# Two paddings that shift the activation tiles x and t by 192 and 384 bytes in SBUF

## The chip, the cores and the metric

The kernel runs on one core of one Trainium2 chip. The metric is the device time of one execution in microseconds (us), lower is better. The time before is the median of three runs, 1311.45 us (1309.43 to 1313.15).

## The reference, cut to what matters

The program is a stack of two blocks on 256 tokens (272 with 16 meta tokens in the first block) of 1,024 features, in float32. The first block is two hybrid layers, the second a feed-forward network, a mixer with a state-space branch, a cross attention and a second feed-forward network. Nearly all of the arithmetic lies in products of an activation with a weight matrix:

```
proj = jnp.einsum('btd,de->bte', h, w_in)            # each of the two hybrid layers
gate, up = jnp.split(u @ w_gate_up, 2, axis=-1)      # each of the two feed-forward networks
return (jax.nn.silu(gate) * up) @ w_down
```

## The kernel before

**Products in three parts.** An activation lies with features on the partitions and tokens along the free axis, in tiles of four blocks `[128, 4, n]`, where n is 272 tokens in the two layers and 256 after them. To keep float32 accuracy with the faster float32r matmul, a weight and an activation are each split into two float32r parts that add up to them: `wh` and `wl`, and a high and a low tile of the activation. One block of 128 rows and 128 columns of a weight matrix then takes three matmuls (`mm3`, lines 217 to 219): `wh` times high, `wh` times low, `wl` times high. `product` runs K such blocks into one PSUM region. In each of them the weight part is the stationary operand (128 columns of 4 bytes, 512 bytes per partition) and the activation the moving one (n columns of 4 bytes, so 1,024 or 1,088 bytes per partition). Each matmul has its own weight load, which stands in the profile under PEld.

**Weights.** `load_w` (L179) brings 1 MB of weights on SyncE's queue into one of three buffers `w`. `split_w` makes the parts of half a buffer: ScalarE copies it into `wh` (L195), VectorE subtracts into `wl` (L197). Five halves of parts are held, so ScalarE and VectorE work ahead of TensorE.

**Who is moving.** The normalized input of the layers, of the two gate-and-up products (44 weight tiles), of the first products of the mixer and of the query product is in tiles named x, from pool `xp`. Everything else that is multiplied by weights is in tiles named t, from pools `tp1` and `tp2`. In the value product of the cross attention (L1053 to L1055) the roles are exchanged: two neighbouring blocks of `wh` or `wl` are moving, 1,024 bytes, and a part of t is stationary. L1021 multiplies a t tile by a t tile.

**Where the tiles lie.** Pools are laid out in SBUF in the order in which they are opened, each partition alike: `cp` (constants), `wp` (3 x 8,192 bytes of `w`, 5 x 4,096 of `wh`, 5 x 4,096 of `wl`), `xp` (4 x 4,352), `sp`, `sm`, and then `tp1` with `lp` (first block) or `tp2` with `mp` (second block). In the built program the first `wh` starts at byte 60,256, the first `wl` at 80,736, the first x at 101,216 and the first t at 138,656. Modulo 256 that is 96 for all weight parts and all x, and 160 for all t: x lies 0 bytes and t 64 bytes from the weight parts, modulo 256. A block of a weight part is 512 bytes and a block of a tile of 256 tokens is 1,024, so in the second block of the program every matmul of `mm3` has the same distance, 0 with x and 64 with t. A block of 272 tokens is 1,088 bytes, which is 64 modulo 256: in the two layers the four blocks of a tile run through the four distances 0, 64, 128, 192 in turn. At L1053 to L1055 the moving operand lies at 96 and the stationary at 160, a distance of 192.

**Order.** The program's order is fixed by the order of the code; side work (attention, the state-space chunks, norms) is written as generators, and `product` takes a step of it at its end.

Of the kernel before, what the change touches and what calls it, by code (L numbers as in the profile page):

```python
# [10 lines left out]
F32 = mybir.dt.float32  # L11
# [7 lines left out]
P = 128  # L19
# [5 lines left out]
EPS = 1e-6  # L25
# [30 lines left out]
def plan():  # L56
    """The weight tiles in the order of their use: name, index, blocks of 128 rows and columns."""
    out = []
    for l in range(2):
        out += [(f"in{l}", i, 16) for i in range(19)]  # L60
        out += [(f"yab{l}", i, 16) for i in range(4)]
        out += [(f"out{l}", i, 16) for i in range(4)]
    out += [("gu1", i, 16) for i in range(NFF)]
    out += [("dn1", i, 11) for i in range(16)]
    out += [("in2", i, 16) for i in range(8)] + [("dt", 0, 8)] + [("in2", i, 16) for i in range(8, 40)]
    out += [("oa", i, 16) for i in range(4)]
    out += [("os", i, 16) for i in range(8)]
    out += [("mx", i, 16) for i in range(4)]
    out += [("kv", i, 16) for i in range(4)]
    out += [("wq", i, 16) for i in range(4)]  # L70
    out += [("kv", i, 16) for i in range(4, 8)]
    out += [("wo", i, 16) for i in range(4)]
    out += [("gu2", i, 16) for i in range(NFF)]
    out += [("dn2", i, 11) for i in range(16)]
    return out
# [3 lines left out]
def tile_hybrid_stack(ctx: ExitStack, tc: tile.TileContext, a: dict, out: bass.AP):  # L79
# [3 lines left out]
    cp = ctx.enter_context(tc.tile_pool(name="cp", bufs=1))  # L83
    wp = ctx.enter_context(tc.tile_pool(name="wp", bufs=2))
    xp = ctx.enter_context(tc.tile_pool(name="xp", bufs=4))
    sp = ctx.enter_context(tc.tile_pool(name="sp", bufs=4))
    sm = ctx.enter_context(tc.tile_pool(name="sm", bufs=4))
# [50 lines left out]
    def load_first():  # L138
        """The inputs and the first weights in the order in which they are needed."""
        w = wp.tile([P, 16, P], F32, tag="w", name=nm("w"), bufs=AHEAD)  # L140
        src = a["in0"][0].rearrange("p (b c) -> p b c", c=P)
        nc.sync.dma_start(vec, a["vec"])
        for i in range(4):
            nc.sync.dma_start(hT[:, 2 * i:2 * i + 2], a["xT"][:, 2 * i:2 * i + 2])
            nc.sync.dma_start(w[:, 4 * i:4 * i + 4], src[:, 4 * i:4 * i + 4])
        return w

# [1 line left out]
    side = []  # L149
# [14 lines left out]

# [1 line left out]
    tiles = plan()  # L166
# [34 lines left out]
    def block(name):  # L201
        """The next block of weights."""
        h = st["half"]
        if h < 0 or st["blk"] == halves[h][2] - halves[h][1]:
            st["half"], st["blk"] = h + 1, 0
            parts.pop(h, None)
            h += 1
            while st["split"] < min(h + PARTS, len(halves)):
                split_w()
        assert tiles[halves[h][0]][0] == name, (tiles[halves[h][0]], name)  # L210
        st["blk"] += 1
        return [x[:, st["blk"] - 1] for x in parts[h]]
# [8 lines left out]
    def wide(ws, part):  # L221
        """Two neighbouring blocks as one operand."""
        x, _ = ws[0][part], ws[1][part]
        return bass.AP(tensor=x.tensor, offset=x.offset, ap=[list(x.ap[0]), [1, 2 * P]])

    def product(o, name, x, K):
        """o = the sum of K blocks of the weights, each times a part of x."""
        for k in range(K):
            mm3(o, name, x(k), k == 0, k == K - 1)
        pump(rate[0])  # L230

    def quads(hi, lo, n=None, t0=0):
        """The parts of block k in tiles of four blocks."""
        return lambda k: (hi[k // 4][:, k % 4, t0:n], lo[k // 4][:, k % 4, t0:n])

    def split_x(hi, lo, src, scale=None):
        """hi + lo == src (times a per-partition scale)."""
        if scale is None:
            A.activation(hi, src, AF.Copy)  # L239
            V.tensor_sub(lo, src, hi.bitcast(F32))  # L240
        else:
            A.activation(hi, src, AF.Copy, scale=scale)
            V.scalar_tensor_tensor(lo, src, scale, hi.bitcast(F32), op0=OP.mult, op1=OP.subtract)  # L243

    def rsqrt(src, n, scale):
        """(src * scale + EPS) ** -0.5 for a few columns."""
        x, t, y = small(n), small(n, I32), small(n, I32)
        V.tensor_scalar(x, src, scale, EPS, op0=OP.mult, op1=OP.add)
        V.tensor_scalar(t, x.bitcast(I32), 1, None, op0=OP.logical_shift_right)
        V.tensor_scalar(y, t, -1.0, MAGIC, op0=OP.mult, op1=OP.add)  # L250
        y = y.bitcast(F32)
        for _ in range(3):
            s, r, z = small(n), small(n), small(n)
            V.tensor_mul(s, y, y)
            V.scalar_tensor_tensor(r, s, -0.5, x, op0=OP.mult, op1=OP.mult)
            V.scalar_tensor_tensor(z, r, 1.5, y, op0=OP.add, op1=OP.mult)
            y = z
        return y

    # token tiles: column, first token of the statistics' rows, first token, tokens  # L260
    TILES1 = [(1, META, META, P), (2, META + P, META + P, P), (0, 0, 0, META)]
    TILES2 = [(0, 0, 0, P), (1, P, P, P)]

    def spread(o, r, tiles):
        """Columns over tokens to rows that all partitions hold."""
        for col, _, s, m in tiles:
            PE.matmul(o[:, s:s + m], r[:m, col:col + 1].to_broadcast([m, P]), ident[:m, :m], start=True, stop=True)  # L267

    class Norm:
        """RMS norm over features of an activation [P, 8, n]: the parts of the activation times  # L270
        the gain, and the reciprocal root of the mean square of each token."""

# [40 lines left out]

# [1 line left out]
    ident_b = cp.tile([P, P], BF16, name="ident_b")  # L315

    def layer(l, nrm, nxt):
# [9 lines left out]

        # keys (index and attention), values and index weights
        ps = project(0)
# [38 lines left out]

        # index queries
        def rope(dst, raw):  # L370
            """Two blocks of two heads, turned."""
            ps = pair()
# [28 lines left out]

        # the choice of keys by the index scores
        mb = {}
# [41 lines left out]

        # queries
        q = t4()
# [10 lines left out]
        def finish_q():  # L458
            """The queries' own norm, of each token and head."""
            c0 = 1 if t0 else 0  # L460
            n = 3 - c0
# [15 lines left out]

        # gates: twice the silu
        def gate():
# [9 lines left out]

        # attention over the chosen keys  # L490
        at_h, at_l = t4(dt=F32R), t4(dt=F32R)
# [75 lines left out]

        # pooling over trailing windows of 2, 4, 8, 16 tokens
        u = t4()
# [41 lines left out]

        # merge gates: twice the sigmoid less one
        tm = [t4() for _ in range(4)]
# [49 lines left out]

# [1 line left out]
    phase["tp"] = ctx.enter_context(tc.tile_pool(name="tp2", bufs=20))  # L665
# [30 lines left out]

# [1 line left out]

# [6 lines left out]

    # the normalized activation, for all but the first products
    def normalize():
# [22 lines left out]
    def conv4(c0):  # L730
        """Four blocks of the convolved channels from c0: twice their silu."""
        y, r = t4(S), t4(S)
# [20 lines left out]

    # steps: softplus(raw + bias), on tokens x heads
    dp_ = bank()
# [33 lines left out]
    V.tensor_scalar(dts, dt, 0.125, None, op0=OP.mult)  # L789
    # sums of la up to each token of its chunk  # L790
    acs_d = dp.tile([2, 32, P], F32, name="acs_d")
# [28 lines left out]
    def ssd(g):  # L820
# [11 lines left out]
        for c in range(2):  # L832
# [9 lines left out]
            yield  # L842
        # the first chunk's state, and the second chunk's view of it
        A.activation(ab, ab, AF.Exp)
# [79 lines left out]

    # short convolution branch
    sh, sl = two(S), two(S)
# [43 lines left out]

    # the memory, for the cross attention
    mem = two(S, F32)
# [22 lines left out]

# [1 line left out]
    drain()  # L997
# [20 lines left out]
    def three(o, w, x, start, stop):  # L1018
        """o = the product of two operands in parts."""
        for i, (a_, b_) in enumerate(((0, 0), (0, 1), (1, 0))):  # L1020
# [70 lines left out]

# [1 line left out]
def _pack(w, blocks, m):  # L1093
    """[K, N] -> [tiles, P, m * K/P * P]: tiles of m blocks of columns, P rows of K on partitions."""
    k = w.shape[0] // P
# [5 lines left out]
def _fp(x):  # L1101
    """[n * P] -> [P, n]"""
    return x.reshape(-1, P).T
# [117 lines left out]
```

## Time and profile before

| what | value |
|---|---|
| median of three runs | 1311.45 us |
| runs | 1309.43, 1313.15, 1311.45 us |
| span of the profiled execution, first to last instruction | 1305.1 us |
| TensorE matmul (PE), weight load (PEld) busy | 97%, 93% of the span |
| VectorE (DVE), ScalarE (ACT), GpSimd (POOL) busy | 71%, 50%, 16% |
| mean granted TensorE clock, share of full | 0.990 |
| HBM read, mean rate over the span | 209.47 MB, 161 GB/s |

The page gives the profiled execution's own time as its span; what a run has beyond it, 6.35 us at the median, lies around the program. Matmuls overlap in the pipeline, so the duration shown for one (near 280 ns) is not what it costs. What it costs is the step from its start to the start of the next, and that is read from start times or from the count of matmuls in a stretch without a gap.

### The profile page before, as it was taken

Reading aid. Unit: us, or ns where it says so; the run is one execution under the profiler, and the core shown is the slowest. Engines: PE = TensorE matmul, PEld = TensorE weight load, DVE = VectorE, ACT = ScalarE, POOL = GpSimd, SP = SyncE. Lnnn points to the kernel's source line nnn. Section 1 sums busy time; section 2 is a strip of 40 time slices with the busy share of each in tenths; the row PEclk is TensorE's granted clock in tenths of the full one; section 3 lists DMA queues with packets and bytes.
Section 4 is the critical chain, followed back from the end, with each engine's and each line's share of the span. In section 5 each row is a group of like instructions: output and inputs, shape, how many; then the busy total and the mean of one; then the engine's idle time right before and its main releaser. Section 6 shows DMA issues by size and latency. Waiting matters only on the chain.

```text
span 1305.1 us, 24570 instructions
## 1 busy us (share of the span) xinstructions
PE 1265.1 (97%) x10202; PEld 1211.9 (93%) x10202; DVE 928.6 (71%) x1526; ACT 654.4 (50%) x973; POOL 209.2 (16%) x165
## 2 busy tenths in 40 slices
PE   7999999999999999999999999999999999999996
PEld 6988689998679899999999999899999999999996
DVE  6698467769647676766678798777778677777653
ACT  5344554444554544445566644455456455444452
POOL 3141022224103100000002333330003001000011
PEclk9999999999899999999999999999999999999998
DMA  7433235443215545545654565454555544555451
GB/s 271 150 130 130 97 105 168 156 162 130 97 65 184 171 162 194 176 142 182 230 180 144 196 224 181 154 184 162 193 195 194 166 157 139 185 175 181 144 189 55
DMA packets 32975, 212.13 MB, mean 163 GB/s; under 512 B 3664, under 2 KB 3792, under 8 KB 11232
## 3 DMA queue, kind: packets, MB, share of 16 engines
q1 hardware_dynamic: 31104, 204.77, 45.7%
q0 software_dynamic: 1184, 4.23, 0.9%
q8 instruction: 80, 1.31, 0.4%
q10 hardware_dynamic: 576, 1.57, 0.4%
q14 instruction: 31, 0.25, 0.1%
HBM read 209.47 MB, written 1.08 MB: 161 GB/s over the span
## 4 chain that ended last, share of the span: by engine, by line
PE 79%; DVE 12%; ACT 3%; issue 3%; POOL 2%; DMA 1%; DVEq 0%; SPq 0%; ACTq 0%; POOLq 0%
PE bank L217 19%; PE bank L218 18%; PE bank L219 18%; PE pair L217 5%; PE pair L218 5%; PE pair L219 5%; DVE wl L197 4%; ACT wh L195 2%; PE aux L519 2%; PE aux L500 1%; DVE acc L418 1%; DVE acc L425 1%; PE aux L516 1%; DVE sm L424 1%; PE aux L267 1%
## 5 line engine op out<-in xcount | busy, mean ns | idle before, releaser
L197 DVE TENSOR_TENSOR wl<-w,wh 128x1024 fp32r<-128x1024 f32 (+3 forms) x406 | 494.4, 1220 | 206.6 <-ACT wh L195 203.9
L195 ACT ACTIVATE wh<-w 128x1024 fp32r<-128x1024 f32 (+3 forms) x406 | 410.7, 1015 | 454.0 <-PE bank L218 303.1
L217 PE MATMUL bank<-t,wh 128*128 128x256 f32 x1320 | 372.0, 282 | 0.4 <-ACT t L239 0.4
L219 PE MATMUL bank<-t,wl 128*128 128x256 f32 x1320 | 367.9, 279 | 0.0
L218 PE MATMUL bank<-t,wh 128*128 128x256 f32 x1320 | 367.8, 279 | 0.0
L217 PEld LDWEIGHTS bank<-t,wh 128*128 128x128 f32 x1320 | 248.0, 188 | 1.8 <-issue 0.8
L218 PEld LDWEIGHTS bank<-t,wh 128*128 128x128 f32 x1320 | 247.4, 187 | 0.7 <-issue 0.7
L219 PEld LDWEIGHTS bank<-t,wl 128*128 128x128 f32 x1320 | 247.7, 188 | 0.0
L217 PE MATMUL bank<-x,wh 128*128 128x256 f32 x832 | 235.8, 284 | 1.2 <-DVE hT L644 1.2
L218 PE MATMUL bank<-x,wh 128*128 128x256 f32 x832 | 235.7, 283 | 0.0
L219 PE MATMUL bank<-x,wl 128*128 128x256 f32 x832 | 235.4, 283 | 0.0
L217 PE MATMUL pair<-x,wh 128*128 128x272 f32 (+1 forms) x608 | 183.6, 302 | 9.4 <-ACT wh L195 7.8
L219 PE MATMUL pair<-x,wl 128*128 128x272 f32 (+1 forms) x608 | 178.6, 294 | 0.9 <-DVE wl L197 0.9
L218 PE MATMUL pair<-x,wh 128*128 128x272 f32 (+1 forms) x608 | 178.5, 294 | 0.0
L217 PEld LDWEIGHTS bank<-x,wh 128*128 128x128 f32 x832 | 159.6, 192 | 1.2 <-ACT wh L195 1.2
L218 PEld LDWEIGHTS bank<-x,wh 128*128 128x128 f32 x832 | 159.7, 192 | 0.1
L219 PEld LDWEIGHTS bank<-x,wl 128*128 128x128 f32 x832 | 159.7, 192 | 0.0
L298 POOL TENSOR_TENSOR ss<-ss,s 128x256 f32<-128x256 f32 (+1 forms) x48 | 45.9, 960 | 604.4 <-ACT s L296 604.1
L217 PEld LDWEIGHTS pair<-x,wh 128*128 128x128 f32 x608 | 118.2, 195 | 13.5 <-ACT wh L195 8.0
L219 PEld LDWEIGHTS pair<-x,wl 128*128 128x128 f32 x608 | 118.2, 194 | 1.6 <-DVE wl L197 1.4
L218 PEld LDWEIGHTS pair<-x,wh 128*128 128x128 f32 x608 | 118.1, 194 | 0.8 <-DVE x L243 0.2
L217 PE MATMUL pair<-t,wh 128*128 128x272 f32 (+1 forms) x256 | 73.4, 288 | 3.5 <-DVE hT L644 2.4
(259 smaller groups left out, 1617.9 us busy)
## 6 DMA issues: line engine op xcount, KB each, us to landing
w<-in_in SPq DMA_DIRECT2D x77, 1024.0 KB, 4.9
w<-in_gu SPq DMA_DIRECT2D x44, 1024.0 KB, 4.9
w<-in_dn SPq DMA_DIRECT2D x32, 704.0 KB, 4.1
w<-in_yab SPq DMA_DIRECT2D x8, 1024.0 KB, 4.9
w<-in_out SPq DMA_DIRECT2D x8, 1024.0 KB, 5.0
w<-in_os SPq DMA_DIRECT2D x8, 1024.0 KB, 4.9
w<-in_kv SPq DMA_DIRECT2D x8, 1024.0 KB, 4.9
t<-acs_d POOLq DMA_DIRECT2D x8, 512.0 KB, 5.4
```

The source lines that it names most:

```text
L195: A.activation(hi[:, b:b + step], w[:, b:b + step], AF.Copy)
L197: (G if slow else V).tensor_sub(lo[:, b:b + step], w[:, b:b + step], hi[:, b:b + step].bitcast(F32))
L217: PE.matmul(o, wh, xh, start=start, stop=False)
L218: PE.matmul(o, wh, xl, start=False, stop=False)
L219: PE.matmul(o, wl, xh, start=False, stop=stop)
L267: PE.matmul(o[:, s:s + m], r[:m, col:col + 1].to_broadcast([m, P]), ident[:m, :m], start=True, stop=True)
L298: G.tensor_add(self.sum, self.sum, self.last)
L418: V.scalar_tensor_tensor(acc[:, :nk], x[:, :nk], wcol, acc[:, :nk], op0=OP.mult, op1=OP.add)
L424: V.max(out=m8, in_=acc[:, :nk])
L425: V.match_replace(out=acc[:, :nk], in_to_replace=m8, in_values=acc[:, :nk], imm_value=MARK)
L500: PE.matmul(lg[:, :nk], q[64 * e:64 * e + 64, i, s0:s0 + P], kk[64 * e:64 * e + 64, 1, :nk], start=True, stop=False)
L519: PE.matmul(po[64 * e:64 * e + 64], vt[:m, c, :HD], ptt[:m], start=c == 0, stop=c == qt)
```

## The change

Two pools of one tile of 48 float32 (192 bytes per partition) are opened, one ahead of `xp` and one behind it. Nothing reads or writes the two tiles. All that lies behind moves up: x by 192 bytes, and `sp`, `sm`, t, `lp` and `mp` by 384 bytes. In the built program of the change x starts at 101,408 and t at 139,040, both 32 modulo 256, while `wh` and `wl` stay at 96. The distance of x and of t from the weight parts is then 192 modulo 256 (at L1053 to L1055 it becomes 64, since there the roles are exchanged). Two t tiles keep their distance from each other, and so do t and the tiles of `lp` (such as `kk`). Every engine's instructions and their order stay as they are. The rest of the diff takes out comments and docstrings.

```diff
     cp = ctx.enter_context(tc.tile_pool(name="cp", bufs=1))
     wp = ctx.enter_context(tc.tile_pool(name="wp", bufs=2))
+    before_x = ctx.enter_context(tc.tile_pool(name="before_x", bufs=1))
+    before_x.tile([P, 48], F32, name="pad_x")
     xp = ctx.enter_context(tc.tile_pool(name="xp", bufs=4))
+    after_x = ctx.enter_context(tc.tile_pool(name="after_x", bufs=1))
+    after_x.tile([P, 48], F32, name="pad_s")
     sp = ctx.enter_context(tc.tile_pool(name="sp", bufs=4))
     sm = ctx.enter_context(tc.tile_pool(name="sm", bufs=4))
```

## Rows read from the trace of the kernel before

**Rows 1.** The page: busy share, and the chain that ended last, by engine.

```profile
PE 1265.1 (97%) x10202; PEld 1211.9 (93%) x10202; DVE 928.6 (71%) x1526; ACT 654.4 (50%) x973; POOL 209.2 (16%) x165
...
PE 79%; DVE 12%; ACT 3%; issue 3%; POOL 2%; DMA 1%; DVEq 0%; SPq 0%; ACTq 0%; POOLq 0%
```

**Rows 2.** TensorE by line and form: count, busy us, mean ns, idle before.

```profile
L217 PE MATMUL bank<-t,wh 128*128 128x256 f32 x1320 | 372.0, 282 | 0.4 <-ACT t L239 0.4
L217 PE MATMUL bank<-x,wh 128*128 128x256 f32 x832 | 235.8, 284 | 1.2 <-DVE hT L644 1.2
...
L217 PE MATMUL pair<-x,wh 128*128 128x272 f32 x352 | 107.5, 305 | 9.4 <-ACT wh L195 7.8 <-DVE mp L538 1.0 <-DVE r L377 0.6
...
L217 PE MATMUL pair<-x,wh 128*128 128x256 f32 x256 | 76.2, 298 | 0.0
...
L1053 PE MATMUL bank<-wh,t 128*128 128x256 f32 x64 | 18.2, 284 | 0.0
```

**Rows 3.** Stretches: length, busy us and count by engine, clock, DMA share, GB/s.

```profile
464.00:575.00 111.00, 111.00 (x928) 111.00 (x927) 79.09 (x90) 49.88 (x59) 0.00 (x0) 1.00 0.49 169
576.00:638.00 62.00, 62.00 (x528) 62.00 (x528) 40.39 (x50) 32.35 (x49) 4.78 (x6) 1.00 0.61 202
835.30:848.40 13.10, 13.10 (x118) 13.10 (x118) 13.10 (x28) 6.32 (x9) 3.28 (x1) 1.00 0.43 136
1119.00:1230.00 111.00, 111.00 (x928) 111.00 (x927) 78.63 (x90) 49.78 (x58) 0.00 (x0) 1.00 0.50 169
```

**Rows 4.** Stretches with products of t, TensorE alone: length, busy us, count.

```profile
744.30:758.00 13.70, 13.70 (x123) 1.00 0.80 295
781.50:792.50 11.00, 11.00 (x99) 1.00 0.52 177
826.30:831.00 4.70, 4.70 (x44) 1.00 0.56 193
832.10:834.40 2.30, 2.30 (x23) 1.00 0.83 223
835.30:848.40 13.10, 13.10 (x118) 1.00 0.43 136
861.60:872.00 10.40, 10.40 (x94) 1.00 0.50 159
1079.80:1101.30 21.50, 21.50 (x192) 1.00 0.44 147
```

**Rows 5.** Timeline of the value product, its first stretch: start us, duration.

```profile
1042.61 0.28 PE L1053 MATMUL bank<-wh,t 128*128 128x256 f32 x1
...
1044.73 0.88 PE L1021 MATMUL aux<-t,t 128*128 128x256 f32 x6
```

**Rows 6.** Timeline of the value product, a later stretch.

```profile
1045.80 0.28 PE L1053 MATMUL bank<-wh,t 128*128 128x256 f32 x1
...
1047.16 0.28 PE L1053 MATMUL bank<-wh,t 128*128 128x256 f32 x1
...
1047.50 0.87 PE L1021 MATMUL aux<-t,t 128*128 128x256 f32 x6
```

**Rows 7.** Timeline of a product of x in the second layer.

```profile
300.16 0.28 PE L217 MATMUL pair<-x,wh 128*128 128x256 f32 x1
...
300.51 0.28 PE L217 MATMUL pair<-x,wh 128*128 128x256 f32 x1
...
300.87 0.28 PE L217 MATMUL pair<-x,wh 128*128 128x256 f32 x1
...
301.58 0.28 PE L217 MATMUL pair<-x,wh 128*128 128x256 f32 x1
```

**Rows 8.** Waits from 446 us on: engine and line, waited for, total us, times, longest.

```profile
ACT wh L195 <- PE bank L218: 303.1, 214, 5.9
...
PE bank L866 <- POOL t L845: 3.4, 2, 2.4
...
SPq L179 <- DVE wl L197: 717.2, 136, 12.0
```

## The prediction

> **What bounds the kernel now.** I read the page first: TensorE is busy 97% of the span and holds 79% of the chain that ended last [rows 1]. Then the waits after the two layers: the largest is ScalarE waiting for a matmul to free a buffer of weight parts, 303.1 us; SyncE's queue waits for VectorE to free a load buffer; TensorE's own longest wait totals 3.4 us [rows 8]. So from about 446 us on the supply of weights runs ahead, and the time is the number of matmuls times the step from one start to the next. The groups by line give the numbers: 832 per line with x and 1,320 with t, three lines each, so 2,496 steps with x and 3,960 with t, and 64 for each of L1053 to L1055, 192 together [rows 2].
>
> Next I read the step, from the count in stretches without a gap. A count includes matmuls that began up to 0.28 us ahead of the stretch, two or three, so some 2.4 are taken off.
> - x, distance 0: (928 - 2.4) matmuls in 111 us are **120.0 ns** each; the second feed-forward network gives the same 928 in 111 us [rows 3].
> - t, distance 64, first down product: (528 - 2.4) in 62 us are **117.9 ns** [rows 3].
> - t, distance 64, elsewhere: seven stretches hold 123, 99, 44, 23, 118, 94 and 192 matmuls [rows 4]. The last gives 21.5 us / 189.6 = **113.4 ns**.
>
> So at one distance, with the same instructions, there are two steps, a long one near 117.8 and a short one near 113.3, and each holds once it is entered. The seven short stretches sum to 693, less 17 for their edges 676, which is 17% of 3,960. The mean at 64 is then 0.17 x 113.3 + 0.83 x 117.8 = 117.0 ns. At distance 0 the 120 ns holds through both long stretches. [...]
>
> **What the new distance does.** Distance 192 with 256 columns in a steady run exists in the trace in one place, the value product. Its first stretch runs 18 matmuls from 1042.61 to 1044.73: 2.12 us / 18 = 117.8 ns, the long step [rows 5]. A later stretch runs twelve from 1045.80 to 1047.16: 1.36 / 12 = 113.3 ns, the short step [rows 6]; the stretches behind it are like it. So 192 shows the same two steps as 64 and never 120, but with the shares turned round: past the first stretch (18 of 192, and a step or two behind each interruption) the short step holds, about three quarters of the 192.
>
> **The change, part by part.**
> - *Added or removed instructions:* none, and no wait is added; the pads cost no time.
> - *The two layers:* unchanged within a few tenths of a us. Four neighbouring blocks already run through all four distances; adding 128 or 192 to each only turns the circle. One turn of twelve matmuls takes 301.58 - 300.16 = 1.42 us, 118.3 ns a step [rows 7], before and after.
> - *x after the layers:* from 120.0 to 117.8 (long) saves 2.2 x 2,496 = 5.5 us; to 113.3 (short) saves 6.7 x 2,496 = 16.7 us.
> - *t after the layers:* from a mean of 117.0 to 117.8 loses 0.8 x 3,960 = 3.2 us if all goes long; to 113.3 saves 3.7 x 3,960 = 14.7 us.
> - *L1053 to L1055:* from three quarters short to somewhere between all short and all long: at most -0.2 or +0.7 us.
> - *Matmuls of t by t and of t by `kk`:* both operands move alike, nothing.
>
> With a share s of short steps after the change the sum is a gain of about 1.6 + 29.4 x s us: 1.6 at s = 0, 31 at s = 1. What is unknown is s. The bounds from rows are 0.17 (distance 64, 3,960 steps) and 0.75 (distance 192, 192 steps). The row at the very distance is nearer in kind, but its stretches are short and all are entered in the same way, behind six matmuls of t by t; the long runs here are entered from waits and from the norm's small matmuls, as at 64. I take the middle, **s = 0.5**: x saves 4.45 x 2,496 = 11.1, t saves 1.45 x 3,960 = 5.7, L1053 gives 0.2 back: **16.6 us**. Against the profiled span that is 1305.1 - 16.6 = 1288.5; with the 6.35 us around the program at the median of the runs, 1311.45 - 16.6 = **1295 us**.
>
> **What hides or eats it.** The cover of the weight supply gets thinner but stays: in the first feed-forward stretch VectorE is busy 79.09 and ScalarE 49.88 of 111 us [rows 3]; with the same work in 105 us (113.3 ns) VectorE is at 75%. In the mixer there is a place where VectorE is busy for the whole 13.1 us of a stretch [rows 3]; a shorter TensorE step gains nothing wherever VectorE lags by more than the parts held ahead. I count no loss for it, since that stretch already runs at the short step; a loss there would be a part of the mixer's share of the 5.7 us. The loads keep waiting for buffers, not the other way [rows 8].
>
> [...]
>
> **Rivals.**
> - *A. Mixed* (s from 0.25 to 0.75): gain 9 to 24 us, 1288 to 1303. For it: both distances with a steady run show both steps.
> - *B. Short nearly everywhere* (s over 0.75): gain 24 to 31, 1280 to 1288. For it: at 192 every stretch after the first is short [rows 6], and once short a run of 190 stayed so [rows 4]; with x and t at one distance there is no more change of distance between them that could end it. Against: the first stretch [rows 5].
> - *C. Long nearly everywhere* (s under 0.25): gain 1.6 to 9, 1303 to 1310. For it: at 64 the long step holds in 83%, and the two feed-forward runs, a third of the steps, depend on two entries.
> - *D. No effect of the distance*: 1311. The step differs with the tile for another reason, such as the use of four x tiles. Against: the two steps within t itself, and the turned roles at L1053 that follow the same two numbers.
> - *E. Slower.* A steady run of `mm3` at 192 locks into the 120 ns that x has at 0. For it: in the second layer the three matmuls of one block take 0.36 us, 120 ns each, from 300.51 [rows 7], and by the order of the program that block lies at 192. Against: the value product at 192 never does. Then x gains nothing, t loses 3.0 x 3,960 = 11.9 us, and the time is 1323. It decides as soon as the mean step with both tiles at 192 is over 118.2 ns, the mean now, (2,496 x 120.0 + 3,960 x 117.0) / 6,456.
>
> **How the numbers follow.** A 0.45, B 0.27, C 0.17, D 0.04, E 0.07. A measurement of this kernel tells a change of about 0.3%, 3.9 us, from none; C passes that bound for s over 0.08, so 0.05 of its 0.17 is "same". Faster: 0.45 + 0.27 + 0.12 = 0.84; same: 0.05 + 0.04 = 0.09; slower: 0.07. The range leaves out E, D and the upper end of C above, and the last of B below: 1281 to 1307. A alone spans 1288 to 1303.
>
> **What the changed profile would show.** In the stretch of the first gate-and-up product, about 928 matmuls in 105 us if short, 109 if long, 111 under D and E. In the down product behind it, 62 us as now if long, under 60 if short. The step should not change between those two products, since x and t now have one distance. In the layers nothing, up to 446 us. At L1053, still two steps. The prediction is wrong if a third step appears at 192 for the order `wh`, `wh`, `wl`, if the step changes in the layers, or if TensorE begins to wait for L195 or L197 after 446 us.

## The result, and the profile after

The changed kernel takes 1290.57 us (median of 4 runs, 1288.71 to 1294.17) against 1312.3 us for the kernel before (4 runs): a ratio of 0.9841, 95% interval 0.9822 to 0.9861. The forecast was 1295 us, with 1281 to 1307 as its range. The profiled execution took 1288.71 us, its span is 1286.6 us against 1305.1. Here and in every listed run 2 us lie around the span; of the 6.35 us that were put there ahead of the prediction, the other 4 are the distance of the profiled execution of the kernel before from its median.

First the page and the waits from 449 us on (the lines of the program lie four further down: L221 to L223 are `mm3`, L199 and L201 make `wh` and `wl`, L1057 to L1059 are the value product).

```profile
PE 1244.2 (97%) x10202; PEld 1191.7 (93%) x10202; DVE 928.8 (72%) x1526; ACT 655.3 (51%) x973; POOL 210.4 (16%) x165
```

```profile
ACT wh L199 <- PE bank L222: 296.7, 223, 5.3
```

```profile
PE bank L870 <- POOL t L849: 2.9, 2, 2.4
```

VectorE, ScalarE and GpSimd are as busy as in [rows 1], within 1.2 us; only TensorE's time is less. The supply of weights still runs ahead, and TensorE's longest wait is as short as in [rows 8]. So the gain is in the step itself. The stretches that answer to [rows 3], with a long run of t in the mixer between them (length, busy us and count of PE, PEld, DVE, ACT, POOL, clock, DMA share, GB/s):

```profile
466.60:570.00 103.40, 103.40 (x915) 103.40 (x914) 77.22 (x90) 50.32 (x58) 0.00 (x0) 1.00 0.53 181
571.50:633.50 62.00, 62.00 (x549) 62.00 (x549) 42.01 (x52) 34.19 (x51) 4.77 (x6) 1.00 0.63 209
696.50:731.50 35.00, 35.00 (x299) 35.00 (x299) 27.44 (x38) 21.71 (x35) 11.30 (x6) 1.00 0.44 151
...
1109.50:1213.00 103.50, 103.50 (x916) 103.50 (x915) 77.49 (x90) 50.32 (x58) 0.00 (x0) 1.00 0.53 181
1214.00:1273.00 59.00, 59.00 (x523) 59.00 (x522) 30.51 (x39) 28.41 (x44) 6.37 (x6) 1.00 0.45 148
```

With 2.4 taken off each count for the edges, as before: the gate-and-up product of x runs at 103.4 / 912.6 = **113.3 ns** where it ran at 120.0, and the down product of t behind it at 62 / 546.6 = **113.4 ns** where it ran at 117.9. The second network does the same. The third row is the long step, 35 / 296.6 = 118.0 ns, which the mixer still has in places.

Where the 18.5 us of span came from, by the start times of all matmuls (steps under 135 ns, those that no wait and no other matmul lengthens): x from a mean of 119.96 to 113.76 ns, 6.2 x 2,496 = 15.5 us; t from 117.00 to 115.09, 1.91 x 3,960 = 7.6 us. From the first product after the layers to the last matmul the kernel before took 850.0 us and this one 828.9, 21.1 less. The layers ended 2.7 us later, at 449.9 instead of 447.2 us.

### The profile page after: what moved, and what is told of

The parts are those of the page before. It is cut to its first block, busy times and chain, and to the rows that moved or that the text cites. A ratio compares the mean times of both kernels' runs of the same rounds, so it can differ in the third digit from the quotient of the medians.

```text
span 1286.6 us, 24570 instructions
## 1 busy us (share of the span) xinstructions
PE 1244.2 (97%) x10202; PEld 1191.7 (93%) x10202; DVE 928.8 (72%) x1526; ACT 655.3 (51%) x973; POOL 210.4 (16%) x165
## 4 chain that ended last, share of the span: by engine, by line
PE 79%; DVE 11%; ACT 3%; issue 3%; POOL 2%; DMA 1%; DVEq 0%; SPq 0%; ACTq 0%; POOLq 0%
PE bank L221 18%; PE bank L222 18%; PE bank L223 18%; PE pair L221 5%; PE pair L223 5%; PE pair L222 5%; DVE wl L201 4%; ACT wh L199 2%; PE aux L523 2%; PE aux L504 1%; DVE acc L422 1%; PE aux L520 1%; DVE acc L429 1%; DVE sm L428 1%; PE aux L1025 1%
## 5 line engine op out<-in xcount | busy, mean ns | idle before, releaser
L201 DVE TENSOR_TENSOR wl<-w,wh 128x1024 fp32r<-128x1024 f32 (+3 forms) x406 | 492.9, 1216 | 190.1 <-ACT wh L199 185.3
L199 ACT ACTIVATE wh<-w 128x1024 fp32r<-128x1024 f32 (+3 forms) x406 | 410.7, 1015 | 425.8 <-PE bank L222 296.7
L221 PE MATMUL bank<-t,wh 128*128 128x256 f32 x1320 | 370.7, 281 | 0.7 <-ACT t L243 0.7
L223 PE MATMUL bank<-t,wl 128*128 128x256 f32 x1320 | 367.2, 278 | 0.0
L221 PEld LDWEIGHTS bank<-t,wh 128*128 128x128 f32 x1320 | 248.7, 188 | 2.2 <-ACT t L243 0.9
L223 PEld LDWEIGHTS bank<-t,wl 128*128 128x128 f32 x1320 | 247.9, 188 | 0.0
L221 PE MATMUL bank<-x,wh 128*128 128x256 f32 x832 | 230.5, 277 | 1.2 <-DVE hT L648 1.2
L222 PE MATMUL bank<-x,wh 128*128 128x256 f32 x832 | 230.4, 277 | 0.0
L223 PE MATMUL bank<-x,wl 128*128 128x256 f32 x832 | 230.0, 276 | 0.0
L221 PE MATMUL pair<-x,wh 128*128 128x272 f32 (+1 forms) x608 | 183.8, 303 | 9.9 <-ACT wh L199 8.3
L223 PE MATMUL pair<-x,wl 128*128 128x272 f32 (+1 forms) x608 | 178.8, 294 | 0.9 <-DVE wl L201 0.9
L221 PEld LDWEIGHTS bank<-x,wh 128*128 128x128 f32 x832 | 156.3, 188 | 1.2 <-ACT wh L199 1.2
L222 PEld LDWEIGHTS bank<-x,wh 128*128 128x128 f32 x832 | 156.3, 188 | 0.2 <-DVE x L247 0.2
L223 PEld LDWEIGHTS bank<-x,wl 128*128 128x128 f32 x832 | 156.2, 188 | 0.0
L221 PEld LDWEIGHTS pair<-x,wh 128*128 128x128 f32 x608 | 118.3, 195 | 14.0 <-ACT wh L199 8.5
L223 PEld LDWEIGHTS pair<-x,wl 128*128 128x128 f32 x608 | 118.2, 194 | 1.6 <-DVE wl L201 1.4
L221 PE MATMUL pair<-t,wh 128*128 128x272 f32 (+1 forms) x256 | 73.5, 289 | 3.5 <-DVE hT L648 2.4
```

The costliest lines, as they stand in the source:

```text
L199: A.activation(hi[:, b:b + step], w[:, b:b + step], AF.Copy)
L201: (G if slow else V).tensor_sub(lo[:, b:b + step], w[:, b:b + step], hi[:, b:b + step].bitcast(F32))
L221: PE.matmul(o, wh, xh, start=start, stop=False)
L222: PE.matmul(o, wh, xl, start=False, stop=False)
L223: PE.matmul(o, wl, xh, start=False, stop=stop)
```

## The experiments

The pads are the only handle: `a` float32 ahead of x and `b` behind it set the two distances. In each diff the minus lines are the changed kernel's. All ratios are to the kernel before on the same chip, whose medians there lie from 1310.05 to 1312.3 us; the mean step is that of the steps under 135 ns of x and t after the layers, from the start times of the profiled execution.

| run | distance of x, t | median us | ratio, 95% interval | mean step, ns |
|---|---|---|---|---|
| before | 0, 64 | 1312.3 | 1 | 118.15 |
| changed | 192, 192 | 1290.57 | 0.9841, 0.9822 to 0.9861 | 114.57 |
| shifted by 256 | 0, 64 | 1310.53 | 1.0, 0.998 to 1.0019 | 118.10 |
| x alone | 192, 64 | 1298.43 | 0.9904, 0.9874 to 0.9933 | 116.71 |
| t alone | 0, 192 | 1303.49 | 0.9944, 0.9924 to 0.9965 | 116.99 |
| both 64 | 64, 64 | 1306.45 | 0.996, 0.9942 to 0.9978 | 117.32 |
| both 0 | 0, 0 | 1319.18 | 1.0071, 1.0049 to 1.0093 | 119.93 |
| both 128 | 128, 128 | 1311.14 | 0.9998, 0.9978 to 1.0018 | 118.66 |
| both 160 | 160, 160 | 1311.18 | 0.9996, 0.9973 to 1.002 | 118.45 |
| both 224 | 224, 224 | 1310.93 | 1.0005, 0.9985 to 1.0025 | 118.33 |
| changed, again | 192, 192 | 1297.62 | 0.9897, 0.9875 to 0.9919 | 115.44 |
| other order | 192, 192 | 1302.33 | 0.9923, 0.9897 to 0.9948 | 117.29 |
| wl at 64 | 192 to wh, 64 to wl | 1285.73 | 0.9806, 0.9784 to 0.9828 | 113.51 |
| wl at 192 | 64 to wh, 192 to wl | 1302.13 | 0.9911, 0.9879 to 0.9943 | 117.25 |

**Is it the distance, or the shift?**

```diff
-    before_x.tile([P, 48], F32, name="pad_x")
+    before_x.tile([P, 64], F32, name="pad_x")
...
-    after_x = ctx.enter_context(tc.tile_pool(name="after_x", bufs=1))
-    after_x.tile([P, 48], F32, name="pad_s")
```

> One pad of 256 bytes ahead of x, none behind it: x and t move as far as a full turn of 256, and their distances from the weight parts stay 0 and 64. If the distance modulo 256 is the cause: the time of the kernel before, 1312 us, a step of 120.0 ns in the gate-and-up products and a mean near 117.0 ns with t. If the shift itself, or what the tiles lie next to, made the gain: 1285 to 1300 us.

Measured 1310.53 us, a ratio of 1.0. Moving x and t by a whole turn of 256 bytes does nothing; the gain doesn't come from the shift, nor from the pads' presence.

**Each tile alone.** The x tile at 192 and t at 64 (`a` = 48, `b` = 16), then x at 0 and t at 192 (`a` = 0, `b` = 32):

```diff
-    after_x.tile([P, 48], F32, name="pad_s")
+    after_x.tile([P, 16], F32, name="pad_s")
```

> Only x goes to distance 192 (pads of 192 and 64 bytes), t stays at 64. My theory (two steps at 64 and at 192, a third of 120.0 ns only at 0): x at 113.3 to 117.8 ns, so 5.5 to 16.7 us less than before, 1296 to 1307, and t between 113.3 and 117.8 ns with a share of its own. If 192 alone favours the short step: x near 113.8 as in the changed kernel, t still near 117.0, 15 us less than before, about 1297. If t is pulled along because x no longer hands over from 120 ns steps: also t near 115, about 1290.

```diff
-    before_x = ctx.enter_context(tc.tile_pool(name="before_x", bufs=1))
-    before_x.tile([P, 48], F32, name="pad_x")
...
-    after_x.tile([P, 48], F32, name="pad_s")
+    after_x.tile([P, 32], F32, name="pad_s")
```

> Only t goes to distance 192 (one pad of 128 bytes behind x), x stays at 0. Theory: x keeps 120.0 ns. The first down product is entered from the 120 ns step of x, as the value product was in the kernel before, where it then ran the long step: so t long there, 117.8 ns, and the gain comes from the mixer alone: 0 to 6 us less than before, 1306 to 1312. If 192 favours the short step whatever runs ahead: t at 115.1 as in the changed kernel, 7.6 us less, about 1304, with both down products short.

x alone: 1298.43 us, ratio 0.9904. t alone: 1303.49, ratio 0.9944. The two gains, 0.0096 and 0.0056, add to 0.0152, near the 0.0159 of both together. A second measurement of both gives 0.0103 (below), so it is not shown that they simply add. The stretches of x alone, TensorE only (length, busy, count, clock, DMA share, GB/s), are the two gate-and-up products and the first down product between them:

```profile
471.00:574.00 103.00, 103.00 (x911) 1.00 0.53 182
576.00:637.00 61.00, 61.00 (x520) 1.00 0.59 199
1119.00:1227.00 108.00, 108.00 (x919) 1.00 0.50 174
```

The same product of the same shapes runs at 103 / 908.6 = 113.4 ns in the first network and at 108 / 916.6 = 117.8 in the second. Over the 1,480 steps of a network that is some 6.6 us, one source of the spread of this kernel's executions, 1294.23 to 1305.39 us. The granted clock may be another: its mean was 0.984 in the slowest of the six and 0.991 in the fastest. In the profiles before and after it is lowest in the two layers, 0.90 and 0.91 from 300 to 360 us; from 450 to 1280 us its mean is 1.00 in both. And in t alone:

```profile
470.00:580.00 110.00, 110.00 (x920) 1.00 0.50 170
581.50:640.00 58.50, 58.50 (x518) 1.00 0.61 206
```

x keeps 110 / 917.6 = 119.9 ns, and t behind it takes the short step, 58.5 / 515.6 = 113.5. My theory said the long one, since the value product of the kernel before had come out of 120 ns into the long step [rows 5]. That one entry was no rule.

**Both at 64, and both at 0.** (`a` = 16, `b` = 48; `a` = 0, `b` = 48.)

```diff
-    before_x.tile([P, 48], F32, name="pad_x")
+    before_x.tile([P, 16], F32, name="pad_x")
```

> Both x and t at distance 64 (pads of 64 and 192 bytes). If 64 and 192 are alike and what counts is that x and t have the same distance, other than 0: about the time of the changed kernel, 1285 to 1297, with long runs of the short step in the feed-forward products. If 192 is better than 64: x at 117 to 117.8 ns and t at 117.0, some 6 us less than before, 1303 to 1308.

> x and t both at distance 0 from the weight parts (one pad of 192 bytes behind x). If the distance is the whole cause: t locks into the 120.0 ns that x has, 3.0 x 3,960 = 12 us more than before, 1321 to 1324, and both feed-forward networks run at 120.0 ns from end to end. If the 120 ns belongs to the x tiles and not to their place: t stays near 117 ns and the time at 1310.

Both at 64 gives 1306.45 us, ratio 0.996: 192 is better than 64, though both have the same two steps. In the profile at 64:

```profile
470.00:578.00 108.00, 108.00 (x919) 1.00 0.50 174
1083.00:1104.00 21.00, 21.00 (x188) 1.00 0.44 151
1121.00:1230.00 109.00, 109.00 (x928) 1.00 0.50 172
```

Both networks are long, 117.8 ns; 1083 to 1104 us is short, 21 / 185.6 = 113.1. A tenth of all steps is 115 ns or less here, and 72% in the changed kernel. Both at 0 gives 1319.18 us, slower than before (1.0049 to 1.0093), and t is now locked at 62.5 / 520.6 = 120.1 ns:

```profile
582.50:645.00 62.50, 62.50 (x523) 1.00 0.58 198
```

The 120 ns goes with the place, not with the tile. The time missed: 1321 to 1324 had been expected, and the median is 1319.18, though the profiled execution took 1325.04.

**Other distances.** (`b` = 48 in all, `a` = 32, 40 and 56.)

```diff
-    before_x.tile([P, 48], F32, name="pad_x")
+    before_x.tile([P, 32], F32, name="pad_x")
```

> x and t both at distance 128. In the two layers a step at 128 is as long as one at 0 (127.1 ns at 272 columns, against 125 at 64 and 192), which speaks for 120 ns and 1320 us. If only 0 has the third step: two steps as at 64 and 192, 113.3 to 117.8 ns, 1280 to 1309 us.

> x and t both at distance 160, half a step of 64 from 192. If what counts is which 64 bytes an operand starts in: like 128, as 160 lies in the same 64 bytes. If it changes smoothly: between 128 and 192. If 192 is a single good place: 117 to 118 ns and 1305 to 1310 us. Open; no number of mine is better than 1280 to 1320.

> x and t both at distance 224, half a step of 64 behind 192. If what counts is which 64 bytes an operand starts in: as at 192, 1285 to 1295 us with three quarters of the steps short. If it changes smoothly: between 192 (mean 114.6 ns) and 0 (120.0 ns), near 117.3 ns and 1308 us.

All three are 1311 us, the same as before within 0.3%. At 128 and at 224 neither 113.3 nor 120.0 ns is held: a stretch of each shows 100 / 842.6 = 118.7 and 100 / 845.6 = 118.3 ns, and by the start times its single steps change between 115 and 123 ns.

```profile
470.00:570.00 100.00, 100.00 (x845) 1.00 0.51 175
```

```profile
470.00:570.00 100.00, 100.00 (x848) 1.00 0.52 179
```

At 160 there are three means, each held through a run: 100 / 842.6 = 118.7, 33.5 / 285.6 = 117.3, and in the third row, by the start times, 120.0 ns.

```profile
470.00:570.00 100.00, 100.00 (x845) 1.00 0.52 179
708.50:742.00 33.50, 33.50 (x288) 1.00 0.44 156
841.50:854.50 13.00, 13.00 (x111) 1.00 0.39 126
```

So neither "128 is like 0" nor "224 is like 192" holds; 32 bytes from 192 on either side the gain is gone.

**The same kernel again, and another order.** The changed kernel as it is, and the second and third line of `mm3` exchanged:

```diff
-        PE.matmul(o, wh, xl, start=False, stop=False)
-        PE.matmul(o, wl, xh, start=False, stop=stop)
+        PE.matmul(o, wl, xh, start=False, stop=False)
+        PE.matmul(o, wh, xl, start=False, stop=stop)
```

> The changed kernel once more, with a second profile. If each run of products takes the long or the short step at its entry and keeps it, by how the entry happens to fall: a median of 1288 to 1293 with a spread of some 6 us and more between executions (one feed-forward network of 1,584 steps is worth 7 us between its two steps), and a second profile with the same two steps but not in all the same places. If the place in the program fixes it: the same stretches short and long as in the first profile, and a spread of 2 to 3 us.

> Both tiles at 192, with the order of the three products changed to wh by high, wl by high, wh by low; all distances modulo 256 stay. If the distance alone sets the steps: 113.3 and 117.8 ns as before and 1285 to 1297 us. If the order counts too (the high tile then moves twice in a row, and the parts wh, wl, wh alternate): another step, or another share; slower where wl comes late.

Again, the kernel takes 1297.62 us (5 runs, 1294.93 to 1301.14), 0.9897 of before; the two measurements of one kernel don't overlap in their intervals. The clock is not the reason, 0.987 to 0.993 here and 0.987 to 0.989 there. The second profile shows most of it: its first network is long (first two rows), its second short, and of the 8.7 us that it is longer after the layers 5.6 are the mean step, 0.87 x 6,456.

```profile
466.00:574.00 108.00, 108.00 (x919) 1.00 0.51 174
575.00:636.00 61.00, 61.00 (x520) 1.00 0.60 199
1117.00:1221.00 104.00, 104.00 (x920) 1.00 0.52 180
```

108 / 916.6 = 117.8 and 104 / 917.6 = 113.3 ns. So a run of products takes one of the two steps at its entry and keeps it, through the change from x to t as well, and which one isn't fixed by the place in the program. Over both profiles the share of short steps is 72% and 53%. With the other order the same two steps appear (107 / 907.6 = 117.9 ns in the first network), but the share falls to 11% and the time rises to 1302.33:

```profile
463.00:570.00 107.00, 107.00 (x910) 1.00 0.51 175
```

So the order leaves the steps as they are. That it lowers the share is suggested and not shown: it is one profile, the share differs between profiles of one kernel too, and the intervals of the ratios, 0.9897 to 0.9948 and 0.9875 to 0.9919 for the changed kernel beside it, overlap.

**The two weight parts at different distances.** A pad of 128 bytes between the `wh` and the `wl` buffers, and x and t moved so that they are at 192 from `wh` and 64 from `wl` (`a` = 16, `b` = 48), then the mirror (`a` = 48, `b` = 48):

```diff
         hi = wp.tile([P, 8, P], F32R, tag="wh", name=nm("wh"), bufs=PARTS)
+        if st["split"] == 0:
+            wp.tile([P, 32], F32, tag="padw", name="pad_w", bufs=1)
         lo = wp.tile([P, 8, P], F32R, tag="wl", name=nm("wl"), bufs=PARTS)
```

> A pad of 128 bytes between the wh and the wl buffers: x and t at 192 from wh and at 64 from wl. If each step goes by the distance of its own operands, and 64 and 192 have the same two steps: 113.3 to 117.8 ns, a share between those of 64 (0.1) and 192 (0.7), 1290 to 1305 us. If a steady run needs one distance throughout: steps that differ by their place among the three, a mean of 118 ns as in the layers, where the distance changes all the time, 1308 to 1313 us.

> The mirror of the run with wl at 64: x and t at 64 from wh and at 192 from wl. If it is the difference of 128 between the two weight parts that takes the long step away: short nearly everywhere again, 113.3 to 113.8 ns, 1284 to 1289 us. If wh, in two of three products, sets the share and 192 favours the short step: mostly long as with both at 64, 117.3 ns, 1302 to 1308 us.

With `wl` at 64: 1285.73 us, 0.9806 of before, below the changed kernel in both of its measurements, and with four runs from 1284.43 to 1287.51 us. Its profile:

```profile
468.00:571.00 103.00, 103.00 (x911) 1.00 0.53 182
573.00:631.00 58.00, 58.00 (x515) 1.00 0.61 207
...
1067.00:1087.00 20.00, 20.00 (x179) 1.00 0.46 159
1105.00:1209.00 104.00, 104.00 (x921) 1.00 0.53 180
```

Every stretch is short: 113.4, 113.1, 113.3 and 113.2 ns. 97% of all steps of x and t after the layers are 115 ns or less, and no run of x or t holds the long step in this profile. The mirror doesn't do this: its first stretch is 106 / 891.6 = 118.9 ns, 29% of its steps are short, and its ten runs lie anywhere from 1285.47 to 1306.42 us (the ratio counts the nine up to 1304.71). One of them is as fast as with `wl` at 64, but it was not profiled.

```profile
466.00:572.00 106.00, 106.00 (x894) 1.00 0.50 173
```

So a steady distance isn't needed for the short step, and a difference of 128 between the two parts alone doesn't bring it. The other reading of the mirror, that `wh`, in two of three products, sets the share and 192 favours the short step, met its numbers: 117.25 ns against 117.3 and 1302.13 us in 1302 to 1308. It doesn't say why `wl` at 64 does better than `wl` at 192, nor why the long run of the mirror is 118.9 and not 117.8 ns. The version with `wl` at 64 is the best of all that ran.

## Why the prediction was right

- **The bound** was read rightly: after the layers the time is the number of matmuls times the step. The granted clock was 1.00 in all stretches of [rows 3] and [rows 4], with 120.0, 117.9 and 113.4 ns, and in those of the profile after, so the steps don't differ by it. The mean step of the table orders the kernels almost as their medians do, and 118.15 - 114.57 = 3.58 ns over 6,456 steps is 23.1 us by the step alone. This part became 21.1 us shorter. By the start times the 6,394 steps under 135 ns became 22.8 us shorter, while the value product became 0.3 us longer, the 62 steps of x and t over 135 ns 0.7, and all other matmuls with their waits 0.7.
- **x**: forecast 120.0 to 115.55, 11.1 us; measured 113.76 ns, 15.5 us. In the second profile it is 115.67 ns, 10.7 us.
- **t**: forecast 117.0 to 115.55, 5.7 us; measured 115.09 ns, 7.6 us. In the second profile it is 115.30 ns, 6.7 us.
- **L1053 to L1055**: forecast a loss of 0.2, at most 0.7. It lost 0.3 us in all, 0.5 in the steps under 135 ns: at 64 they now run mostly long. Six steps from 1042.99 us take 0.70 us, 117 ns each, where a later stretch of [rows 6] had 113.3.

```profile
1042.99 0.28 PE L1057 MATMUL bank<-wh,t 128*128 128x256 f32 x1
...
1043.69 0.28 PE L1057 MATMUL bank<-wh,t 128*128 128x256 f32 x1
```

- **The share s.** The one free number, taken as 0.5 between 0.17 and 0.75, was 0.72 in the first profile and 0.53 in the second. The lower bound was the wrong one for 192: the 0.17 belongs to 64, and both at 64 stayed there (0.10) when x had joined t. The row at the very distance, from 192 matmuls of another product, was the better guide, and other profiles bear it out: the value product is short in 62 to 75% of its steps in the four kernels that have it at 192, and in at most 10% in the four with all its operands at 64. The middle itself had no row behind it. Measured once the kernel beat the forecast by 4 us, measured again it missed it by 3, so that 1295 came so near is in part luck.
- **One step through x and t** was forecast, and held: from 466 to 634 us more than 1,470 matmuls in a row keep the short step across the handover.
- **The layers** should not change. One turn of twelve still takes 301.72 - 300.30 = 1.42 us, as in [rows 7]. The steps of 256 columns with x there went from a mean of 117.6 to 118.3 ns, some 0.5 us in all. The rest of the 2.7 us by which the layers ended later is no effect of the distance that could be told: over the fourteen profiles they end anywhere from 446.2 to 454.2 us. The clock is granted differently there, in this profile at 0.97 in the first 60 us and 0.98 from 120 to 180 us where both were 1.00 before, but at 0.99 from 60 to 120 us where it was 0.97; how much that makes isn't settled.

```profile
300.30 0.28 PE L221 MATMUL pair<-x,wh 128*128 128x256 f32 x1
...
301.72 0.28 PE L221 MATMUL pair<-x,wh 128*128 128x256 f32 x1
```

- **The rivals.** D falls with the result itself and with both at 0; the shift by 256 excludes only that the shift itself or the pads made the gain. The medians of the table reach from 1285.73 to 1319.18 us with no instruction changed but for the order in one. E falls: nothing at 192 holds 120 ns; its evidence, blocks of the layers, was no steady run. A (1288 to 1303) and B (1280 to 1288) are not two kinds of kernel but two shares, and the share differs between executions of one kernel (0.72 and 0.53); all nine timed runs of this kernel lie in A.

Why a distance has the steps that it has isn't settled. Shown is which steps each distance holds; a cause inside TensorE or SBUF was not tried apart. Nor did a run move weight parts and tiles together by less than 256 bytes, which would separate the distance from the places of the two operands themselves. Two things speak for the distance. In the kernel before, the moving operand lies at 96 modulo 256 both with x and in the value product; with the stationary one at 96 the step is 120.0 ns, with it at 160 it is 113.3 or 117.8, the two steps that `mm3` has at that distance from other places. And with `wl` at 64, x, t and `wh` lie at the very bytes where the changed kernel has them; the move of `wl` by 128 alone took the share from 72% and 53% to 97%.

## What to carry to other kernels

Where TensorE streams without gaps, count the matmuls in a stretch and divide: here equal shapes at a granted clock of 1.00 had steps of 120.0 ns at distance 0 and of 113.3 or 117.8 at 64 and 192. A pad of a few hundred bytes is a cheap trial: the one of 256 bytes left the time at 1310.53 us, a ratio of 1.0. Try the distances one by one, for moving and for each stationary buffer, since 32 bytes more or less lost the gain here (1310.93 and 1311.18 us) and the best version, 1285.73 us, has the two weight parts at different distances. Where a step is chosen at entry, as at 192 here with 72% and 53% of short steps in two profiles, one profile and four runs don't describe the kernel: look for the layout that leaves no choice, as `wl` at 64 did, and judge it by its spread too.

## What the runs showed of the hardware that was not expected

- The step of a 128x256 float32r matmul with its weight load was 120.0 ns with both operands at one place modulo 256, 113.3 or 117.8 at 64 and at 192, in the mean 118.7 at 128 and 118.3 at 224, and 117.3, 118.7 or 120.0 at 160. At 192 the step was taken at the entry and differed between two executions of one kernel, 113.3 ns in the first gate-and-up product of the first profile and 117.8 in that of the second; once taken it stayed for more than 1,470 matmuls, from 466 to 634 us of the first.
- With both weight parts at 192 the share of the short step was 72% and 53% in two profiles; with `wl` at 64 it was 97% in one, and its four runs lie within 3.1 us.
